# One recurrence step for four heads instead of two groups of two, 16-row products side by side, full value products first

## The chip, the cores and the metric

The kernel runs on one core of a Trainium2 chip. The metric is the device time of one execution in microseconds. Engines: PE (TensorE, the matrix products), PEld (its weight loads), DVE (VectorE), ACT (ScalarE), POOL (GpSimd) and SP (SyncE, which issues the loads of the weights).

## The reference: what is computed

A decoder trunk of two layers on 256 tokens plus 16 learned ones put ahead (272 in all), 1024 wide, float32. A layer is a half-step SwiGLU, a token-mixing part of two branches, and another half-step SwiGLU. The branches are latent attention with 8 heads and a gated linear recurrence (HGRN2) with 4 heads of 128 x 128. The change touches both branches, the second above all:

```python
def step(S, inp):
    qt, kt, vt, gt = inp
    b = jnp.cumsum(gt, axis=2)
    diff = b[:, :, :, None, :] - b[:, :, None, :, :]
    decay = jnp.exp(jnp.where(causal[:, :, None], diff, NEG_BIG))
    attn = jnp.einsum('bhtk,bhtsk,bhsk->bhts', qt, decay, kt) * scale
    o = jnp.einsum('bhts,bhsv->bhtv', attn, vt) + \
        jnp.einsum('bhtk,bhkv->bhtv', qt * jnp.exp(b) * scale, S)
    b_last = b[:, :, -1:, :]
    S = jnp.exp(b_last[:, :, 0, :])[..., None] * S + \
        jnp.einsum('bhsk,bhsv->bhkv', kt * jnp.exp(b_last - b), vt)
    return S, o
...
o = o * lax.rsqrt(jnp.mean(o * o, axis=-1, keepdims=True) + EPS) * norm_w.astype(f32)
gate = jax.nn.silu(g_in.astype(f32)).reshape(B, L, HG_HEADS, HG_VDIM)
return (o * gate).reshape(B, L, HG_WIDTH).astype(dt)
```

## The kernel before, in words

Activations lie feature-major: 128 features on the partitions, 272 tokens along them. In the last layer the 16 learned tokens are no longer needed as queries, and most work there runs on 256 columns.

Every weight is read from memory in float32 and split into an exact high and low part: ACT casts the high part (`wh`, L144), DVE subtracts (`wl`, L145). A wide product is three matrix products per contraction step (`mm3`, L163 to L165), so one output tile of 128 x 272 with 8 steps takes 24. The pieces of weights are prepared two ahead of their use. The other products, in the recurrence and in attention, are plain float32; in the trace one of them counts as two passes of PE.

PSUM has two rings of four tiles, `mm` (wide products) and `aux` (the rest). A tile is given out in the order in which the program asks, so a fifth request waits for the first one's readers.

`mix` (L399 on) is the token-mixing part. It is written as Python generators, dealt out by hand: each `yield` ends a step, and the loops at its end take a step of one, then of another. The recurrence inputs come first (`gq`, `gk`, `gf` for queries, keys and forget factors, two tiles each, one per group of two heads). Then:

- `halving(gr)`, one for each group `gr` of two heads, forms the decayed products by halving. For block sizes 1, 2, 4, 8, 16 `blocks` (products inside 32-token blocks, L714, and for the 16 learned tokens L718) and for 32 and 64 `halves` (L740) multiply keys and queries. Then DVE multiplies half of the queries and of the keys by the totals (L765, L767) before the next size. A last step forms the products between the two tiles of 128 tokens and with the 16 learned tokens (L778, L782). The results are gathered in `at`, `am` and `amm`. That is nine steps for each group.
- `outputs()` multiplies them with the values, head by head: a 16-row product into the 16 learned tokens (L798, not in the last layer), a 16-row product into the other 256 (L799), and two full-array products (L800, L801). Then it squares (L803), sums the squares over each head's features (L811), takes the square root on ACT and the reciprocal on DVE (L284, L285 of `rsqrt`), spreads the factors with one 32-row product for each head (L819), multiplies (L821) and splits (L168, L169).
- `attention()`, head by head, takes scores (L643), maximum, exponential (L648) and transposes (L661 to L663), the transposes of one head behind the scores of the next; at the end, two by two, the products with the values: one of full width (L684) and four that are 64 columns wide (L688), for each pair of heads.

The order around the change: while the four gate products run, one recurrence step follows each; so too for the four steps of `heads()` (attention's queries, keys and values); then `weave` goes round by round: a step of attention, a wide product, a step of the recurrence. The two groups take turns:

```python
rec = chain(alternate(halving(0), halving(1)), outputs())
for _ in tiles(4, cq, done_g):
    pump()
    next(rec)
...
for _ in weave("awr", a=attention(), r=rec, w=rest):
    pass
```

With 18 steps of halving and 5 of outputs, the recurrence takes 23 steps: 4, 4, and 15 rounds of the weave. Which instruction then stands where on an engine is set by a scheduler, which keeps roughly to the order of the program and lets others pass where its estimate says that one would wait.

Of the kernel before, what the change touches and what calls it, by code (L numbers as in the profile page):

```python
# [18 lines left out]
P = 128  # L19
# [3 lines left out]
NM = 16  # L23
# [29 lines left out]
def trunk(ctx: ExitStack, tc: tile.TileContext, a: dict):  # L53
# [28 lines left out]
    # a unit's pieces: (its number, contraction steps, columns)  # L82
# [67 lines left out]
    # the next piece, as a list over its contraction steps  # L150
# [33 lines left out]
    at = [T([P, 2, 3, P], F32, "at", 2) for _ in range(2)]  # L184
    for t in at:
        GP.memset(t, 0.0)
# [22 lines left out]
    # lower bounds of the forget gates, by a softmax over the layers  # L209
# [71 lines left out]
    # in steps, so that other work can stand between them  # L281
# [15 lines left out]
    # two or more output tiles; the last contraction step of all of them comes last  # L297
# [57 lines left out]
    # the last one, token-major, with the norm of the output  # L355
    def ffn_out(norm, c):
# [8 lines left out]
        for hf in range(2):  # L365
            pst = [PS(), PS()]
            for k0 in range(0, NF, 2):
                w = piece()
                for t in range(2):
# [6 lines left out]
                    for k in range(4 if k0 == 0 else 0):  # L376
                        E.matmul(pst[t][:, k * P:(k + 1) * P], h[4 * hf + k][:, slice(*TOK[1 + t])], ident,
                                 start=False, stop=False)
            for t in range(2):
                sq = T([P, 512], F32, "gq", 2)  # L380
                sq = S.activation(out=sq, in_=pst[t], func=AF.Square, accum_out=fm[:, hf, t:t + 1])
            for t in range(2):
                o = T([P, 512], F32, "gk" if hf else "gf", 2)
# [15 lines left out]
    def mix(l, norm, nxt):  # L399
# [12 lines left out]
        # rms_norm(r p) = p rsqrt(mean(p p) + EPS / (r r)), with 1 / (r r) from the outer norm  # L412
# [18 lines left out]
        # latent queries, latent keys and values (each with its norm), the shared rotary key  # L431
# [43 lines left out]
        def heads():  # L475
            kpe = st["kpe"]
            # queries
# [25 lines left out]
            # keys and values  # L503
# [40 lines left out]
        # recurrence inputs  # L544
# [9 lines left out]
        gq = [T([P, 2, L], F32, "gq", 2) for _ in range(2)]  # L554
        gk = [T([P, 2, L], F32, "gk", 2) for _ in range(2)]
# [59 lines left out]
        def attention():  # L615
# [66 lines left out]
            for pr in range(4):  # L682
# [10 lines left out]
                if pr % 2:  # L693
                    yield
# [297 lines left out]
```

## Time and profile before

| | |
|---|---|
| median of 3 runs | 1233.23 us (1232.86 to 1233.68) |
| span of the profiled execution | 1232.4 us |
| PE busy | 1216.2 us |
| DVE busy | 870.1 us |
| ACT busy | 643.7 us |
| instructions | 24345 |
| TensorE clock granted | 0.999 of full speed (2.4 GHz) |

The profiled execution's own time is its span, from its first instruction to its last, with a start and an end around it that the profile doesn't show; the median of the runs is 0.8 us above the span. In the timelines the start of an instruction is the safe number. The ends of PE's products are modelled and overlap, so what a product costs is read from its start to the next one's start.

### The profile page before, as it was taken

The page shows a single profiled execution, that of the slowest core. Times are in us where ns is not written, and L with a number is a line of the kernel's source. Part 1 is how long each engine was busy: PE and PEld are TensorE (multiplying, and loading weights), DVE is VectorE, ACT ScalarE, POOL GpSimd, SP SyncE. Part 2 cuts the span into 40 slices and gives each one's busy share as a digit, 9 for nine tenths or more (in the row PEclk, how much of TensorE's full clock was granted, in tenths as well). Part 3 has the DMA queues.
Part 4 walks back from the last instruction along what each step waited for, and adds up shares of the span by engine and source line. Part 5 has one row for each costly group of instructions (what it writes and reads, how often), then busy time and mean ns, then how long its engine had stood idle before and what let it go on. Part 6 is the DMA issues. An engine that isn't in the chain of part 4 may idle for free.

```text
span 1232.4 us, 24345 instructions
## 1 busy us (share of the span) xinstructions
PE 1216.2 (99%) x10210; PEld 1175.0 (95%) x10210; DVE 870.1 (71%) x1585; ACT 643.7 (52%) x1073; POOL 8.6 (1%) x28
## 2 busy tenths in 40 slices
PE   7999999999999999999999999999999999999997
PEld 6999999999988999999999999999998899999986
DVE  5877755787866877776558776558869586977743
ACT  5544444566774644444445444445776655545442
POOL 0000000000000000000000000000000000000000
PEclk9999999999999999999999999999999999999999
DMA  7645555545332545646555546555454345555651
GB/s 225 204 149 196 177 179 178 173 142 158 122 134 86 189 141 168 201 148 211 163 165 174 183 160 197 187 156 173 140 168 138 120 138 172 191 172 186 206 188 52
DMA packets 188781, 203.50 MB, mean 165 GB/s; under 512 B 3348, under 2 KB 176480, under 8 KB 188672
## 3 DMA queue, kind: packets, MB, share of 16 engines
q1 hardware_dynamic: 188272, 201.36, 50.4%
q8 instruction: 80, 1.31, 0.4%
q10 hardware_dynamic: 400, 0.60, 0.1%
q14 instruction: 29, 0.24, 0.1%
HBM read 200.89 MB, written 1.05 MB: 164 GB/s over the span
## 4 chain that ended last, share of the span: by engine, by line
PE 96%; ACT 2%; DVE 1%; DMA 1%; issue 0%; SPq 0%; POOLq 0%; POOL 0%
PE pmm L163 21%; PE pmm L164 21%; PE pmm L165 21%; PE paux L164 7%; PE paux L165 7%; PE paux L163 7%; PE pmm L373 2%; PE pmm L374 2%; PE pmm L375 2%; PE paux L643 1%; PE paux L714 1%; PE paux L688 1%; DMA raw<-x 1%; ACT wh L144 0%; ACT act L501 0%; PE paux L800 0%
## 5 line engine op out<-in xcount | busy, mean ns | idle before, releaser
L144 ACT CAST wh<-raw 128x1024 fp32r<-128x1024 f32 (+3 forms) x398 | 398.4, 1006 | 388.7 <-PE pmm L164 263.0
L145 DVE TENSOR_TENSOR wl<-raw,wh 128x1024 fp32r<-128x1024 f32 (+3 forms) x398 | 464.4, 1170 | 172.5 <-ACT wh L144 170.7
L163 PE MATMUL pmm<-x,wh 128*128 128x272 f32 (+1 forms) x1312 | 381.1, 291 | 0.7 <-ACT act L513 0.7
L165 PE MATMUL pmm<-x,wl 128*128 128x272 f32 (+1 forms) x1312 | 375.8, 287 | 0.0
L164 PE MATMUL pmm<-x,wh 128*128 128x272 f32 (+1 forms) x1312 | 375.6, 286 | 0.0
L163 PEld LDWEIGHTS pmm<-x,wh 128*128 128x128 f32 x1312 | 246.8, 188 | 3.0 <-ACT act L513 1.0
L164 PEld LDWEIGHTS pmm<-x,wh 128*128 128x128 f32 x1312 | 247.0, 188 | 0.9
L165 PEld LDWEIGHTS pmm<-x,wl 128*128 128x128 f32 x1312 | 246.4, 188 | 0.2
L163 PE MATMUL pmm<-act,wh 128*128 128x272 f32 (+1 forms) x836 | 239.8, 287 | 0.0
L164 PE MATMUL pmm<-act,wh 128*128 128x272 f32 (+1 forms) x836 | 239.1, 286 | 0.0
L165 PE MATMUL pmm<-act,wl 128*128 128x272 f32 (+1 forms) x836 | 238.9, 287 | 0.0
L163 PE MATMUL paux<-x,wh 128*128 128x272 f32 (+1 forms) x704 | 201.1, 286 | 0.0
L164 PE MATMUL paux<-x,wh 128*128 128x272 f32 (+1 forms) x704 | 201.1, 286 | 0.0
L165 PE MATMUL paux<-x,wl 128*128 128x272 f32 (+1 forms) x704 | 201.1, 286 | 0.0
L163 PEld LDWEIGHTS pmm<-act,wh 128*128 128x128 f32 x836 | 157.3, 188 | 1.0 <-issue 0.8
L164 PEld LDWEIGHTS pmm<-act,wh 128*128 128x128 f32 x836 | 157.5, 188 | 0.4 <-issue 0.4
L165 PEld LDWEIGHTS pmm<-act,wl 128*128 128x128 f32 x836 | 157.0, 188 | 0.5 <-issue 0.3
L163 PEld LDWEIGHTS paux<-x,wh 128*128 128x128 f32 x704 | 132.8, 189 | 0.0
L164 PEld LDWEIGHTS paux<-x,wh 128*128 128x128 f32 x704 | 132.6, 188 | 0.0
L165 PEld LDWEIGHTS paux<-x,wl 128*128 128x128 f32 x704 | 132.5, 188 | 0.0
L168 ACT CAST act<-tmp 128x272 fp32r<-128x272 f32 (+1 forms) x88 | 36.5, 415 | 124.4 <-DVE tmp L317 124.4
L313 DVE TENSOR_TENSOR tmp<-pmm,rstd 128x272 f32<-128x272 f32 (+1 forms) x88 | 38.3, 435 | 50.9 <-PE pmm L165 50.6
(239 smaller groups left out, 1058.9 us busy)
## 6 DMA issues: line engine op xcount, KB each, us to landing
raw<-ffn_w_gu SPq DMA_DIRECT2D x86, 1024.0 KB, 5.3
raw<-w_in SPq DMA_DIRECT2D x36, 1024.0 KB, 5.2
raw<-ffn_w_down SPq DMA_DIRECT2D x34, 1024.0 KB, 5.2
raw<-ffn_w_down SPq DMA_DIRECT2D x12, 768.0 KB, 4.9
raw<-w_out SPq DMA_DIRECT2D x8, 1024.0 KB, 5.4
raw<-w_proj_attn SPq DMA_DIRECT2D x4, 1024.0 KB, 5.0
raw<-w_proj_rec SPq DMA_DIRECT2D x4, 1024.0 KB, 5.0
raw<-ffn_w_gu SPq DMA_DIRECT2D x4, 512.0 KB, 9.0
```

What stands on the lines that cost most here:

```text
L144: S.copy(out=hw, in_=x)
L145: V.tensor_tensor(out=lw, in0=x, in1=hw.bitcast(F32), op=ALU.subtract)
L163: E.matmul(ps, wh, xh, start=start, stop=False)
L164: E.matmul(ps, wh, xl, start=False, stop=False)
L165: E.matmul(ps, wl, xh, start=False, stop=stop)
L168: S.copy(out=hi_tile[:, c], in_=src)
L313: V.tensor_tensor(out=gt[:, c], in0=pg[:, c], in1=r[:, c], op=ALU.mult)
L373: E.matmul(pst[t], ah[:, ts_], wh, start=k == 0, stop=False)
L374: E.matmul(pst[t], al[:, ts_], wh, start=False, stop=False)
L375: E.matmul(pst[t], ah[:, ts_], wl, start=False, stop=k == NF - 1)
L643: E.matmul(ps[:, 0:n], qs[hd][0:DQK, TOK[i + 1][0]:TOK[i + 1][1]], kT[hd][0:DQK, 0:n], start=True, stop=True)
L688: E.matmul(ps[j * 64:j * 64 + 64, 16 + i * P:L], vt[1 + i][:, hd * 64:hd * 64 + 64], pts[hd][:, i * 256:256 + i * P], start=False, stop=i ...
```

## The change

Four things are done. `halving` handles all four heads in one step: `gq`, `gk`, `gf`, `at` and the small tiles hold four heads, a visit to `blocks` or `halves` issues the products of four heads, and the instructions of DVE, ACT and POOL behind them are as many as for one group before, on tiles twice as large. The recurrence then has 14 steps in place of 23. `outputs` issues the 16-row products of all four heads first, into four tiles at once (two of `aux`, two of `mm`), and then the full-array ones head by head. In attention two full-width value products come first, and then the eight narrow ones. The last norm's scratch tiles are slices of one tile, since `gq`, `gk` and `gf` have another shape now; the comments are gone.

```diff
-    at = [T([P, 2, 3, P], F32, "at", 2) for _ in range(2)]
-    for t in at:
-        GP.memset(t, 0.0)
+    at = T([P, G, 3, P], F32, "at")
+    GP.memset(at, 0.0)
...
-        gq = [T([P, 2, L], F32, "gq", 2) for _ in range(2)]
-        gk = [T([P, 2, L], F32, "gk", 2) for _ in range(2)]
-        gf = [T([P, 2, L], F32, "gf", 2) for _ in range(2)]
+        gq, gk, gf = (T([P, G, L], F32, n) for n in ("gq", "gk", "gf"))
...
-            for pr in range(4):
-                ps = PS("aux")
-                E.matmul(ps[:, cq], vt[0][:, pr * P:(pr + 1) * P], pmt[:, cq], start=True, stop=False)
-                for i in range(2):
-                    for j in range(2):
...
+            for p2 in range(2):
+                prs = [(2 * p2 + i, PS("aux")) for i in range(2)]
+                for pr, ps in prs:
+                    E.matmul(ps[:, cq], vt[0][:, pr * P:(pr + 1) * P], pmt[:, cq], start=True, stop=False)
+                for pr, ps in prs:
+                    for i in range(2):
+                        for j in range(2):
...
                 ps = PS("aux")
-                pv = ps[:, 0:P].rearrange("p (j t c) -> p j t c", j=2, t=2)
-                for j in range(2):
+                pv = ps[:, 0:2 * P].rearrange("p (g t c) -> p g t c", g=G, t=2)
+                for g in range(G):
                     for ti in range(2):
                         for b in range(4):
                             bs = slice(TOK[2 - ti][0] + 32 * b, TOK[2 - ti][0] + 32 * b + 32)
-                            E.matmul(pv[32 * b:32 * b + 32, j, ti], k[:, j, bs], q[:, j, bs], start=True, stop=True)
+                            E.matmul(pv[32 * b:32 * b + 32, g, ti], k[:, g, bs], q[:, g, bs], start=True, stop=True)
...
                 V.tensor_tensor(out=qv[:, :, :, 1], in0=qv[:, :, :, 1],
-                                in1=first.unsqueeze(3).broadcast_to([P, 2, nq, b]), op=ALU.mult)
+                                in1=first.unsqueeze(3).broadcast_to([P, G, nq, b]), op=ALU.mult)
...
             og, sqs = [], []
+            pss = [PS(t) for t in ("aux", "aux", "mm", "mm")]
+
             for g in range(G):
-                gr, j = divmod(g, 2)
+                ms = slice(32 * g, 32 * g + NM)
+                if not last:
+                    E.matmul(pss[g][:, 0:NM], gv[0][ms], amm[ms], start=True, stop=True)
+                E.matmul(pss[g][:, NM:L], gv[0][ms], am[ms], start=True, stop=False)
+            for g in range(G):
                 gs = slice(g * P, (g + 1) * P)
-                ms = slice(32 * g, 32 * g + NM)
-                ps = PS("aux")
-                if not last:
-                    E.matmul(ps[:, 0:NM], gv[0][ms], amm[ms], start=True, stop=True)
-                E.matmul(ps[:, NM:L], gv[0][ms], am[ms], start=True, stop=False)
-                E.matmul(ps[:, NM:L], gv[1][:, gs], at[gr][:, j, 1:3], start=False, stop=False)
-                E.matmul(ps[:, 144:L], gv[2][:, gs], at[gr][:, j, 0], start=False, stop=True)
+                ps = pss[g]
+                E.matmul(ps[:, NM:L], gv[1][:, gs], at[:, g, 1:3], start=False, stop=False)
+                E.matmul(ps[:, 144:L], gv[2][:, gs], at[:, g, 0], start=False, stop=True)
...
-        rec = chain(alternate(halving(0), halving(1)), outputs())
+        rec = chain(halving(), outputs())
```

How it moves instructions, at two places (the lines are those of each kernel; the changed one's are a few lower). First, PE in the first layer, where the recurrence's outputs are formed; `gv` are the values, `at`, `am` and `amm` the decayed products. Before, for heads 0 and 1:

```order
L798 MATMUL paux_4712<-amm_2545,gv_427_2539 128x16
L799 MATMUL paux_4712<-am_2542,gv_427_2539 128x256
L800 MATMUL paux_4712<-at_69,gv_2540 128x256
L801 MATMUL paux_4712<-at_69,gv_2541 128x128
L798 MATMUL paux_4721<-amm_2545,gv_427_2539 128x16
L799 MATMUL paux_4721<-am_2542,gv_427_2539 128x256
L800 MATMUL paux_4721<-at_69,gv_2540 128x256
L801 MATMUL paux_4721<-at_69,gv_2541 128x128
```

Now, in the same step; the full-array products of heads 2 and 3 follow in the next one, behind a wide product:

```order
L793 MATMUL paux_4181<-amm_2539,gv_423_2534 128x16
L794 MATMUL paux_4181<-am_2537,gv_423_2534 128x256
L793 MATMUL paux_4182<-amm_2539,gv_423_2534 128x16
L794 MATMUL paux_4182<-am_2537,gv_423_2534 128x256
L793 MATMUL pmm_4183<-amm_2539,gv_423_2534 128x16
L794 MATMUL pmm_4183<-am_2537,gv_423_2534 128x256
L793 MATMUL pmm_4184<-amm_2539,gv_423_2534 128x16
L794 MATMUL pmm_4184<-am_2537,gv_423_2534 128x256
L798 MATMUL paux_4181<-at_69,gv_2535 128x256
L799 MATMUL paux_4181<-at_69,gv_2536 128x128
L798 MATMUL paux_4182<-at_69,gv_2535 128x256
L799 MATMUL paux_4182<-at_69,gv_2536 128x128
```

The 16-row products (before L798 and L799, now L793 and L794) of all four heads stand together ahead of the full-array ones, in four tiles, where they stood alternately with them.

Second, ACT in the first layer, where the root of the outputs' norm is taken (`rsqrt`, before L284, now L283). Before, in the stretch behind attention's last exponential (L860 is the sigmoid of the merge gates):

```order
L860 ACTIVATE act_4779<-act_4779 128x272
L803 ACTIVATE tmp_4786<-paux_4781 128x272
L803 ACTIVATE tmp_4795<-paux_4790 128x272
L284 ACT_TABLE_LOAD
L284 ACTIVATE tmp_4843<-tmp_4820 128x272
L144 CAST wh_4926<-raw_4924 128x1024
```

Now, between the exponentials (L645) of attention's heads 3 and 4; L662 copies transposes, L650 scales a head's second tile:

```order
L662 COPY ptt_4296<-paux_4292 128x384
L645 ACTIVATE pm_4274,sm_4038<-paux_4276,sm_4038 128x144
L645 ACTIVATE pm_4275,sm_4038<-paux_4284,sm_4038 128x272
L650 ACTIVATE pm_4275<-pm_4275,sm_4038 128x256
L144 CAST wh_4423<-raw_4362 128x1024
L283 ACT_TABLE_LOAD
L283 ACTIVATE tmp_4394<-tmp_4334 128x272
L645 ACT_TABLE_LOAD
L645 ACTIVATE pm_4337,sm_4038<-paux_4339,sm_4038 128x144
```

The root moved from behind attention into its middle, and a second table load follows it, back to the exponential.

## Rows read from the trace of the kernel before

**Rows 1.** The page, busy time by engine: us, share of the span, instructions.

```profile
PE 1216.2 (99%) x10210; PEld 1175.0 (95%) x10210; DVE 870.1 (71%) x1585; ACT 643.7 (52%) x1073; POOL 8.6 (1%) x28
```

**Rows 2.** The page, the chain that ended last, share by engine.

```profile
PE 96%; ACT 2%; DVE 1%; DMA 1%; issue 0%; SPq 0%; POOLq 0%; POOL 0%
```

**Rows 3.** Timeline of PE, layer 0, first visit to `blocks`: start, us, line, shape, count.

```profile
271.31 0.29 PE L165 MATMUL pmm<-x,wl 128*128 128x272 f32 x1
...
272.80 0.29 PE L165 MATMUL pmm<-x,wl 128*128 128x272 f32 x1
273.01 0.46 PE L714 MATMUL paux<-gq,gk 128*32 128x32 f32 x32
273.29 0.24 PE L718 MATMUL paux<-gq,gk 128*32 128x16 f32 x4
...
273.69 0.29 PE L164 MATMUL pmm<-x,wh 128*128 128x272 f32 x1
```

**Rows 4.** Timeline of PE, layer 0, output products of heads 0 and 1.

```profile
369.04 0.39 PE L801 MATMUL paux<-at,gv 128*128 128x128 f32 x2
369.35 0.39 PE L798 MATMUL paux<-amm,gv 16*128 16x16 f32 x2
369.60 0.67 PE L799 MATMUL paux<-am,gv 16*128 16x256 f32 x2
370.20 0.70 PE L800 MATMUL paux<-at,gv 128*128 128x256 f32 x2
370.74 0.38 PE L801 MATMUL paux<-at,gv 128*128 128x128 f32 x2
370.96 0.62 PE L684 MATMUL paux<-act,vt 128*128 128x272 f32 x2
```

**Rows 5.** Timeline of PE, layer 0, four 32-row products in four row groups.

```profile
389.28 0.74 PE L819 MATMUL paux<-act,cst 32*128 32x272 f32 x8
389.95 0.39 PE L164 MATMUL pmm<-act,wh 128*128 128x272 f32 x1
```

**Rows 6.** Timeline of PE, layer 0, value products of attention.

```profile
361.53 0.73 PE L684 MATMUL paux<-act,vt 128*128 128x272 f32 x2
362.19 0.87 PE L688 MATMUL paux<-ptt,vt 128*64 128x256 f32 x8
362.99 0.73 PE L684 MATMUL paux<-act,vt 128*128 128x272 f32 x2
```

**Rows 7.** Windows of 10 us, layer 0: PE, PEld, DVE, ACT, POOL busy (instructions), clock, DMA.

```profile
270.00:280.00 10.00, 10.00 (x144) 9.58 (x144) 7.47 (x17) 4.82 (x14) 0.00 (x0) 1.00 0.34 107
...
320.00:330.00 10.00, 10.00 (x136) 9.25 (x136) 9.81 (x34) 6.73 (x15) 0.34 (x2) 1.00 0.42 122
...
370.00:380.00 10.00, 10.00 (x64) 7.39 (x63) 3.67 (x7) 2.94 (x6) 0.00 (x0) 1.00 0.01 2
```

**Rows 8.** Groups of DVE by line: busy us, mean ns; idle before.

```profile
L285 DVE RECIPROCAL tmp<-tmp 128x272 f32<-128x272 f32 (+1 forms) x12 | 21.8, 1820 | 1.9 <-ACT tmp L284 1.8
...
L765 DVE TENSOR_TENSOR gq<-gq,tb 128x256 f32<-128x256 f32 (+1 forms) x24 | 10.2, 424 | 0.8 <-PE paux L740 0.7
...
L821 DVE SCALAR_TENSOR_TENSOR act<-paux,cols,act 128x272 f32<-128x272 f32 (+1 forms) x8 | 3.6, 486 | 0.8 <-PE paux L819 0.8
...
L746 DVE TENSOR_TENSOR gq<-gq,gf 128x544 f32<-128x544 f32 (+1 forms) x4 | 2.8, 698 | 0.0
```

**Rows 9.** Timeline of ACT, layer 0: the table load ahead of the square root.

```profile
380.88 1.28 ACT L284 ACT_TABLE_LOAD   x1
382.18 0.43 ACT L284 ACTIVATE tmp<-tmp 128x272 f32<-128x272 f32 x1
```

**Rows 10.** Waits of PE in the mixing stages: us in total, times, longest.

```profile
PE paux L662 <- ACT pm L653: 0.8, 1, 0.8
...
PE pmm L163 <- ACT act L513: 0.7, 1, 0.7
PE paux L643 <- ACT act L514: 0.7, 1, 0.7
```

More of the change, by code (lines that the diff above doesn't have):

```diff
@@ L378, in ffn_out @@
                                  start=False, stop=False)
+            sqs, os = (T([P, 2, 512], F32, n) for n in ("gq", "gk" if hf else "gf"))
             for t in range(2):
-                sq = T([P, 512], F32, "gq", 2)
-                sq = S.activation(out=sq, in_=pst[t], func=AF.Square, accum_out=fm[:, hf, t:t + 1])
+                sq = S.activation(out=sqs[:, t], in_=pst[t], func=AF.Square, accum_out=fm[:, hf, t:t + 1])
             for t in range(2):
-                o = T([P, 512], F32, "gk" if hf else "gf", 2)
+                o = os[:, t]
                 r = fm[:, 2, t:t + 1]
@@ L572, in done_q @@
             S.activation(out=s[:, cq], in_=z[:, cq], func=AF.Sigmoid)
-            V.scalar_tensor_tensor(out=gq[g // 2][:, g % 2, cq], in0=z[:, cq], scalar=P ** -0.5,
+            V.scalar_tensor_tensor(out=gq[:, g, cq], in0=z[:, cq], scalar=P ** -0.5,
                                    in1=s[:, cq], op0=ALU.mult, op1=ALU.mult)
@@ L739, in halves @@
                         for o in starts:
-                            E.matmul(pv[o:o + b, j, ti], k[:, j, t0 + o:t0 + o + b],
-                                     q[:, j, t0 + o + b:t0 + o + 2 * b], start=True, stop=True)
+                            E.matmul(pv[o:o + b, g, ti], k[:, g, t0 + o:t0 + o + b],
+                                     q[:, g, t0 + o + b:t0 + o + 2 * b], start=True, stop=True)
                 for o in starts:
@@ L771, in halving @@
                 yield
-            km = T([P, 2, 32], F32, "km", 2)
-            V.tensor_tensor(out=km, in0=k[:, :, 0:32], in1=tb[:, :, 0:1].broadcast_to([P, 2, 32]), op=ALU.mult)
+            km = T([P, G, 32], F32, "km", 1)
+            V.tensor_tensor(out=km, in0=k[:, :, 0:32], in1=tb[:, :, 0:1].broadcast_to([P, G, 32]), op=ALU.mult)
             ps = PS("aux")
             pmx = PS("aux")
-            for j in range(2):
-                E.matmul(ps[:, j * P:(j + 1) * P], k[:, j, 16:144], q[:, j, 144:272], start=True, stop=True)
+            for g in range(G):
+                E.matmul(ps[:, g * P:(g + 1) * P], k[:, g, 16:144], q[:, g, 144:272], start=True, stop=True)
             for i in range(2):
-                for j in range(2):
-                    o = 64 * gr + 32 * j
-                    E.matmul(pmx[o:o + 32, i * P:(i + 1) * P], km[:, j] if i else k[:, j, 0:32],
-                             q[:, j, 16 + i * P:144 + i * P], start=True, stop=True)
-            S.copy(out=A[:, :, 2, :], in_=ps[:, 0:256].rearrange("p (j c) -> p j c", j=2))
-            S.copy(out=am[hs], in_=pmx[hs, 0:256])
+                for g in range(G):
+                    E.matmul(pmx[32 * g:32 * g + 32, i * P:(i + 1) * P], km[:, g] if i else k[:, g, 0:32],
+                             q[:, g, 16 + i * P:144 + i * P], start=True, stop=True)
+            S.copy(out=A[:, :, 2, :], in_=ps.rearrange("p (g c) -> p g c", g=G))
+            S.copy(out=am, in_=pmx[:, 0:256])
             yield
```

48 lines of the change are left out of this document (23 added, 25 removed).

## The prediction

> **What bounds the kernel now.** Read the busy times first: PE is busy for 1216.2 of 1232.4 us [rows 1]; the other engines have room on the whole. The chain that ended last says the same, PE 96% [rows 2]. So a change pays only where PE issues for a shorter time, or waits less; an instruction saved on DVE or ACT pays nothing by itself. Then read PE's timeline in the two mixing stages (about 270 to 392 us and 880 to 1000 us), start to start, since the modelled ends overlap. Twelve wide products (three per contraction step, 272 columns) take 272.80 - 271.31 = 1.49 us, 0.124 each [rows 3]. What stands between them are small products, and there a start-to-start gap shows more than streaming: whenever PE goes from full-array products to ones on 32-column, 64-column or 16-row parts and back, it pays. Last read the load of DVE by stretch: 7.5 of 10 us while the gate products run, 9.8 in the rounds of attention, 3.7 where the recurrence's outputs stand now [rows 7]. PE waits little there: 0.7 twice for ACT's key copies, and 0.8 once for a transpose's input [rows 10].
>
> The profiled execution is the base of the sum: its span is 1232.4 us, and the median of the runs is 1233.23; I add 0.8 at the end.
>
> **Recurrence in one step for four heads.** The count of products is the same; the 18 visits per layer become 9. One visit now: from the last wide product before it (272.80) to the second behind it (273.69) 0.89 us, less two wide products, 0.64 [rows 3]. Of that, 32 passes take 0.28 (273.01 to 273.29) [rows 3]. A visit for four heads adds 32 passes and costs about 0.64 + 0.28 = 0.92 in place of 1.28. That is 0.36 per pair. In the last layer, which has no 16-column products, the visit is shorter, and for blocks of 32 and 64 tokens and the totals the added passes run on fewer columns at a time, so I take 0.29 per pair: 9 pairs x 2 layers x 0.29 = **5.2 us**. Bounds: 0, if the added passes cost a visit each time; 6.5, at 0.36 throughout.
>
> DVE has half as many instructions, but not half the time: 544 elements take 0.70 us, two instructions of 256 or 272 take 0.85 [rows 8]. The doubled steps now stand one behind the other in the four gate products and in the heads. There a step brings two multiplications and a masked copy, some 1.0 us more per round of 4 us; DVE is idle for 2.5 of 10 us [rows 7], 1.0 per round, so it just fits. I cost it at nothing; if the cover is gone, each of six rounds per layer lengthens by at most the 1.0. Pool's copies and the larger memset come long before they are needed.
>
> **16-row products side by side.** Now each head of the first layer has 0.25 (16 columns) + 0.60 (256 columns, with the way back to the full array) + 0.54 + 0.22, with 0.31 for the last where a 16-row product follows [rows 4]: 1.70, in the last layer without the first, 1.45. Four heads and two layers: 12.6 us. Afterwards four 16-row products stand in four row groups and four tiles. The nearest row is the spread of the head factors: four products of 32 rows and 272 columns take 0.67 together [rows 5], where one product of that width takes 0.47 on the full array (0.22 for 128 columns, scaled) [rows 4]. So they run together. I take 0.67, plus 0.25 once for the 16-column ones. The full products cost 0.22 per 128 columns, 0.66 per head, as no change of shape stands between them. With 0.1 for the one change into row groups: 3.7 and 3.4 us, 7.1 in all, **5.5 us** saved. Bounds: 1.3, if they run one by one; 6.0, if the 16-column ones cost nothing.
>
> **Full value products first.** 361.53 to 362.19 is 0.66 for one full product, of which 0.47 is streaming; the four half-width ones behind it take 0.80 [rows 6], of which about 0.63 is streaming. With two full ones and then eight half ones, one change each way goes, 0.19 + 0.17, at four places: **1.4 us**. Bounds 0 and 1.5.
>
> Together PE saves **12.1 us**.
>
> **What moves.** Before, recurrence steps reached into round 15 behind the start of attention, and the square root, the reciprocal and the norm products fell where DVE has 6 of 10 us free. Now the steps are 14, eight of them before attention starts, and the last five fall into rounds 2 to 6 of attention, DVE's full stretch. Out of these rounds go eight steps with two multiplications of 0.42 [rows 8]. In come per layer a reciprocal of 1.82, four products of 0.49, and 12 plain operations of 0.42 [rows 8], 8.9 us, lumped into two rounds. A round of PE is 24 wide products, 3.0, and one head's scores and transposes, some 1.05 by the columns; with the recurrence's visit, about 0.5 where the shape changes anyway, 4.6. DVE's own work in it is 4.6 x 0.98 [rows 7] less 1.3 of recurrence (two multiplications, a masked copy), 3.2. In the round of the norm products DVE gets 3.2 + 4 x 0.49 + 4 x 0.42 = 6.9 us against PE's 4.05 + 0.67: late by 2.2. In the round of the reciprocal ACT gets two table loads (to the square root and back to the exponential) of 1.28 [rows 9] and the root's 0.43 on top of some 3.1 [rows 7], 6.1 against PE's 5.2: late by 0.9. What is late next: the norm products take all four aux tiles, and the score products behind them on PE wait until DVE frees two; then maximum, exponential and transposes of that head. Part of this 3.1 us is covered, because a head's transposes are asked for a round later and wide products can stand between. I take two thirds, 2.1 per layer, less the old 0.8 which belonged to the same chain: **3.4 us** back. Bounds: 0 less 0.8, and 6.2. The two waits for key copies stay [rows 10].
>
> About the swap the Trainium skill, in "ScalarE: Activation LUTs", section "What ACT_TABLE_LOAD costs", says that each switch of sets costs a load of 1283 ns and a drain of about 1380 ns. The load agrees; the drain does not, as the root starts at 382.18, right where the load ends [rows 9]. By the page's price the two swaps per layer would take 2.76 us more on ACT, and the sum would rise by up to 5.5 us.
>
> The sum: 1232.4 - 12.1 + 3.4 = 1223.7, plus 0.8: **1224.5 us**.
>
> **The rivals.**
> - The waits don't come (wide products cover the lumps): 1232.4 - 12.1 - 0.8 + 0.8 = 1220.3. For it: PE's order puts wide products ahead of the late transposes. Against it: the aux tiles.
> - The 16-row products don't run side by side: 4.2 us less gain, 1228.7. For it: two of them stand on one row group, one behind the other. Against it: rows 5.
> - Doubled visits cost what two cost, so the first part doesn't do what it says: 5.2 less, 1229.7. Against it: 0.28 for 32 passes [rows 3].
> - The swap drains ACT, by a gap behind each load: 5.5 more, 1230.0. Rows 9 show no gap.
> - **Slower**: the norm work inside attention is paid in full. The place is the score products behind the norm products; the price 8.9 us of DVE per layer, 17.8, on 12.1 saved and 0.8 added: 1232.4 - 12.1 + 17.8 + 0.8 = 1238.9. It decides once the new waits pass 12.1 us, over 6 per layer. Against it: as much halving work leaves the same rounds.
>
> **How the numbers follow.** Forecast 0.55 (1221.5 to 1228), no waits 0.17, one by one 0.13, doubled visits 0.06, drain 0.03, slower 0.06. 0.2%, about what a measurement of this kernel can tell from no change, is 2.5 us: under 1230.8 counts as faster. The forecast and the first three rivals lie there but for their upper ends: faster 0.88, within 0.06, slower 0.06. The range, 1219 to 1230.5, takes in the cases on the side of a gain and leaves out the slower one and the upper ends.
>
> **What would show it.** Right: 9 recurrence visits per layer, of about 0.9 us; four 16-row products within about 1 us; two full value products in a row; PE's busy time near 1204; new waits of 2 us or so per layer behind the four norm products. Wrong: 16-row products 0.6 apart; PE waiting more than 6 us per layer for DVE's norm products or for ACT's table loads; or PE stalls among the gate products, where DVE would be the bound.

## The result, and the profile after

The changed kernel takes **1220.88 us** (1220.78 to 1221.88, four runs), the kernel before beside it 1233.3 us (1232.86 to 1233.68, four runs): 12.4 us less, a ratio of 0.9898 with an interval of 0.9886 to 0.9911. The profiled execution has a span of 1218.8 us and a time of 1220.78 us. The page of the kernel after, busy time and the chain by engine (to be read against [rows 1] and [rows 2]):

```profile
PE 1203.2 (99%) x10210; PEld 1170.0 (96%) x10210; DVE 866.9 (71%) x1522; ACT 645.5 (53%) x1067; POOL 8.7 (1%) x19
...
PE 96%; DVE 2%; ACT 1%; DMA 0%; issue 0%; SPq 0%; POOLq 0%; POOL 0%
```

PE still sets the time; it is busy for 13.0 us less with the same 10210 products. The chain has 2% of DVE now where it had 2% of ACT.

A second measure is used below, because medians of this size carry about a microsecond that has nothing to do with the change. The first 2082 products of PE are the same in every kernel here, and yet the first recurrence visit starts between 271.5 and 273.1 us in the kept traces: later where the wide products go over later from 0.23 us apart to 0.12 (15.0 to 18.5 us from the start), or where the first input is late. From the start of that visit to PE's last product the kernel before takes 952.4 us and the changed one 939.3, **13.1 us less**. This stretch is called the traced stretch; each run has one trace.

**The shapes.** PE's timeline in layer 0, kernel after: the first recurrence visit, the output products, one of the two value visits (start, us, line, tiles, shape, count):

```profile
272.42 0.29 PE L165 MATMUL pmm<-x,wl 128*128 128x272 f32 x1
272.63 0.73 PE L711 MATMUL paux<-gq,gk 128*32 128x32 f32 x62
...
273.38 0.39 PE L163 MATMUL pmm<-x,wh 128*128 128x272 f32 x1
273.61 0.29 PE L164 MATMUL pmm<-x,wh 128*128 128x272 f32 x1
...
327.02 0.29 PE L793 MATMUL paux<-amm,gv 16*128 16x16 f32 x2
...
327.26 0.47 PE L794 MATMUL paux<-am,gv 16*128 16x256 f32 x2
327.29 0.47 PE L794 MATMUL pmm<-am,gv 16*128 16x256 f32 x2
327.56 0.39 PE L794 MATMUL paux<-am,gv 16*128 16x256 f32 x2
327.59 0.39 PE L794 MATMUL pmm<-am,gv 16*128 16x256 f32 x2
327.90 0.70 PE L798 MATMUL paux<-at,gv 128*128 128x256 f32 x2
328.44 0.38 PE L799 MATMUL paux<-at,gv 128*128 128x128 f32 x2
...
338.80 0.67 PE L809 MATMUL paux<-tmp,ones 128*32 128x272 f32 x8
339.39 0.39 PE L640 MATMUL paux<-act,act 96*128 96x144 f32 x1
...
364.25 1.08 PE L682 MATMUL paux<-act,vt 128*128 128x272 f32 x4
365.26 1.52 PE L687 MATMUL paux<-ptt,vt 128*64 128x256 f32 x16
366.71 0.39 PE L163 MATMUL pmm<-x,wh 128*128 128x272 f32 x1
```

A four-head visit is 273.61 - 272.42 less two wide products, 0.94, where the pair of visits took 2 x 0.64 [rows 3]. Eight 16-row products take 327.90 - 327.02 = 0.88 for four heads, where one head's took 0.25 + 0.60 [rows 4]. Two full and eight half value products take 2.46 us (364.25 to 366.71) with one change each way, where 361.53 to 362.99 was half of that work in 1.46 [rows 6].

**The waits.** The waits of PE in the mixing stages, kernel after: us in total, times, longest.

```profile
PE paux L640 <- DVE act L819: 1.1, 2, 0.6
PE paux L737 <- DVE gk L764: 0.6, 2, 0.4
PE pmm L163 <- DVE act L605: 0.6, 2, 0.3
PE pmm L165 <- DVE wl L145: 0.4, 2, 0.2
```

None of the waits of [rows 10] is left, and four of another kind stand in their place, 2.7 us together, all for DVE. The first is the one behind the norm products; the other three belong to one step, the recurrence's 32-token step (`halves`, L737) in the round of the keys. PE's timeline there, kernel after, and below it DVE's and GpSimd's:

```profile
302.45 0.57 PE L737 MATMUL paux<-gq,gk 128*32 128x32 f32 x24 [0.22 <-DVE gk L764]
303.25 0.64 PE L165 MATMUL pmm<-act,wl 128*128 128x272 f32 x3 [0.23 <-DVE wl L145]
303.82 0.32 PE L737 MATMUL paux<-gq,gk 128*32 128x32 f32 x8
304.41 0.39 PE L163 MATMUL pmm<-act,wh 128*128 128x272 f32 x1 [0.27 <-DVE act L605]
```

```profile
300.71 0.89 DVE L762 TENSOR_TENSOR gq<-gq,tb 128x512 f32<-128x512 f32 x1
301.52 0.88 DVE L764 TENSOR_TENSOR gk<-gk,tb 128x512 f32<-128x512 f32 x1
302.32 1.68 DVE L145 TENSOR_TENSOR wl<-raw,wh 128x512 fp32r<-128x512 f32 x2
...
306.54 0.68 DVE L762 TENSOR_TENSOR gq<-gq,tb 128x512 f32<-128x512 f32 x1
...
300.62 2.85 POOL L753 COPY at<-cb 32x256 f32<-32x256 f32 x4 [297.85 <-DVE cb L723]
```

Three wide products stand in the middle of the visit, so it pays its changes of shape twice. The windows of the kernel after, in layer 0, for this round and for the round of the norm products (PE, PEld, DVE, ACT, POOL busy, clock, DMA) show DVE full in both.

```profile
296.00:306.00 10.00, 9.28 (x153) 8.46 (x152) 10.00 (x21) 9.12 (x19) 2.67 (x4) 1.00 0.44 117
340.00:350.00 10.00, 10.00 (x80) 9.67 (x82) 10.00 (x28) 8.27 (x17) 0.00 (x0) 1.00 0.32 106
```

Part of that load is GpSimd's doing. Beside its copies (300.62) four DVE instructions on 128 x 512 elements in a row, the two multiplications and two subtractions, take 0.88 to 0.89 us each, where the same sizes take 0.68 to 0.69 without them: 0.8 us per layer, at the very place where PE waits 0.7 us in layer 0 and 0.9 in the last. No run takes the copies away, so it is not shown whether PE would wait without them.

### The profile page after: what moved, and what is told of

Read it like the earlier page. It is cut to its first block, busy times and chain, and to the rows that moved or that the text cites. A ratio compares the mean times of both kernels' runs of the same rounds, so it can differ in the third digit from the quotient of the medians.

```text
span 1218.8 us, 24265 instructions
## 1 busy us (share of the span) xinstructions
PE 1203.2 (99%) x10210; PEld 1170.0 (96%) x10210; DVE 866.9 (71%) x1522; ACT 645.5 (53%) x1067; POOL 8.7 (1%) x19
## 3 DMA queue, kind: packets, MB, share of 16 engines
q8 instruction: 80, 1.31, 0.5%
## 4 chain that ended last, share of the span: by engine, by line
PE 96%; DVE 2%; ACT 1%; DMA 0%; issue 0%; SPq 0%; POOLq 0%; POOL 0%
PE pmm L163 22%; PE pmm L164 21%; PE pmm L165 21%; PE paux L164 7%; PE paux L165 7%; PE paux L163 7%; PE pmm L372 2%; PE pmm L373 2%; PE pmm L374 2%; PE paux L640 1%; DVE wl L145 1%; PE paux L711 1%; DMA raw<-x 0%; PE paux L687 0%; PE pmm L376 0%; PE paux L682 0%
## 5 line engine op out<-in xcount | busy, mean ns | idle before, releaser
L164 PE MATMUL pmm<-x,wh 128*128 128x272 f32 (+1 forms) x1312 | 376.0, 287 | 0.0
L164 PEld LDWEIGHTS pmm<-x,wh 128*128 128x128 f32 x1312 | 247.1, 188 | 1.0
L164 PE MATMUL pmm<-act,wh 128*128 128x272 f32 (+1 forms) x836 | 238.8, 286 | 0.0
L164 PE MATMUL paux<-x,wh 128*128 128x272 f32 (+1 forms) x704 | 201.1, 286 | 0.0
L164 PEld LDWEIGHTS pmm<-act,wh 128*128 128x128 f32 x836 | 157.4, 188 | 0.0
L164 PEld LDWEIGHTS paux<-x,wh 128*128 128x128 f32 x704 | 132.6, 188 | 0.0
```

The lines of the kernel that those rows point to most:

```text
L164: E.matmul(ps, wh, xl, start=False, stop=False)
```

## The experiments

Each group of runs was timed against the kernel before on its own chip (1233.0 to 1233.4 us). Differences between two runs of this list are differences of medians, without an interval of their own; the traced stretch stands beside them where the two disagree.

**The three parts alone.** First the value products only: of the diff above, on the kernel before, the loop in `attention` and nothing else.

> The kernel before with the third part of the change alone: two full-width value products first, then the eight narrow ones. Shape theory (PE's gain comes from fewer changes between full-array and narrow products): each of the four places takes 2.5 to 2.6 us in place of 2.9, so the time falls by about 1.5 us and PE's busy time with it. Rival, waits theory (the gain of the whole change comes from moving the recurrence off attention's rounds, so that PE waits less): no change, within 0.3 us.

1232.04 us, ratio 0.999 (0.9981 to 0.9999): 1.0 us less, with up to 2.3 in the interval; in the traced stretch 1.2. Each of the four places shrinks by 0.34 to 0.36 us, from 6.32 to 5.96 at one of them. Shape, as expected.

Second the output products only, on the kernel before:

```diff
+            pss = [PS(t) for t in ("aux", "aux", "mm", "mm")]
+            for g in range(G):
...
+                E.matmul(pss[g][:, NM:L], gv[0][ms], am[ms], start=True, stop=False)
             for g in range(G):
...
-                E.matmul(ps[:, NM:L], gv[0][ms], am[ms], start=True, stop=False)
+                ps = pss[g]
```

> The kernel before with the second part alone: the 16-row products of all four heads first, into two aux and two mm tiles; the halving stays in two groups. Shape theory: the 16-row products stand within about 0.9 us in the first layer and 0.65 in the last, in place of 3.4 and 2.4, and the time falls by about 5.7 us. Waits theory: less than 1 us. A third outcome, that two of the four mm tiles held over a wide product make PE wait for a tile: the fall is smaller by as much as the waits that then show ahead of wide products.

1229.83 us, ratio 0.9972 (0.9961 to 0.9983): 3.2 us less, in the traced stretch 3.6. The 16-row products stand side by side as in the changed kernel, 0.89 for the eight of layer 0. Part of that gain is lost again behind attention, at two places. The product for the sum of squares comes right behind the last square there, is split in two by a wide product, and pays two changes of shape: 0.8 us per layer. And behind the norm products PE waits for DVE's splits (L164 <- DVE act L169, 0.6 us in two waits), which it reaches earlier now.

Third the recurrence for four heads only: the changed kernel with the old loops in `attention` and `outputs`.

> The changed kernel with the outputs head by head and the value products pair by pair as before, so the four-head halving and its earlier steps alone. Shape theory: a fall of 3.6 us from the visits, 1.1 from the sum of squares which no longer waits for ACT's last square, and 0.8 of new waits, in all about 4 us below the kernel before. Waits theory: this part carries most of the whole change, a fall of 8 us or more.

1227.81 us, ratio 0.9953 (0.994 to 0.9967): 5.2 us less, in the traced stretch 5.9; the waits of [rows 10] are gone, and the four waits of the changed kernel are there. So this part alone exchanges the waits. The three parts give 1.0 + 3.2 + 5.2 = 9.4 us alone and 12.4 together; each interval reaches 1.1 to 1.7 us to either side, so the times don't settle the difference. The traced stretches do say that there is one, 10.8 against 13.1: alone, the output products lose what the paragraph above tells, and in the changed kernel the sum of squares is in one piece and no wait for L169 is left.

**The sum of squares.** In the kernel before, its product L811 takes 1.14 us, start to start; in the changed kernel L809 takes 0.59. PE's timeline in the kernel before, and the wait that its weight loads (PEld) have there:

```profile
380.36 1.20 PE L811 MATMUL paux<-tmp,ones 128*32 128x272 f32 x8
381.50 0.40 PE L163 MATMUL pmm<-act,wh 128*128 128x272 f32 x1
...
PEld paux L811 <- ACT tmp L803: 0.8, 2, 0.4
```

One more `yield` ahead of it, in the kernel before:

```diff
+            yield
             ss = PS("aux")
```

> The kernel before with one more step between the output products and the product that sums their squares, nothing else. If the 1.14 us of that product was mostly a wait for ACT's last square, it takes about 0.6 now and the time falls by about 1 us. If it is what four products in column groups take, it stays at 1.1 and the time stays within 0.3 us.

PE's timeline of this run:

```profile
380.67 0.67 PE L812 MATMUL paux<-tmp,ones 128*32 128x272 f32 x8
381.27 0.39 PE L163 MATMUL pmm<-act,wh 128*128 128x272 f32 x1
```

The product takes 0.60: half of the 1.14 was a wait for ACT's last square, as the first of the two outcomes had it. But the time does not fall: 1232.93 us, ratio 0.9998 (0.9989 to 1.0006), and the traced stretch is 952.4 us in both. PE gains 0.5 us per layer at this place and loses it some 14 us later, where the first products behind the norm products wait for DVE's splits (L164 <- DVE act L169, 0.2 us at 394.78). So behind attention PE can't use the gain: what comes later there is the chain of root, reciprocal, norm products and splits.

**The tiles of the norm products.** The changed kernel with

```diff
-            pss = [PS("aux") for _ in range(G)]
+            pss = [PS(t) for t in ("mm", "mm", "aux", "aux")]
```

> The changed kernel, with one edit: the four products that spread the head factors (L817) take two tiles of mm and two of aux, where they took four of aux. In the changed kernel the score products behind them (L640) wait for DVE's L819, 1.1 us of PE's idle time at two places, and 2.0 us of the weight loads'. Theory A, the prediction's: the wait is for the ring of aux tiles; then it goes, and the time falls by 1.1 to 2.0 us, to about 1219.4 (ratio to the changed kernel 0.9987, to the kernel before 0.989), and no row L640 <- DVE act L819 is left. Theory B: DVE is late with everything in this round, so the wait only moves, to the next tile of mm or to the transposes L658: within 0.5 us of 1220.9, and a new row of 0.5 us or more appears.

1224.66 us (1223.59 to 1225.43), ratio 0.9931 (0.9918 to 0.9945): **3.8 us slower** than the changed kernel, in the traced stretch 4.1, so neither theory holds. The waits of PE, its timeline in the last layer, and the windows:

```profile
PE pmm L817 <- DVE act L288: 2.9, 2, 1.6
PE paux L658 <- DVE act L819: 1.3, 2, 0.8
```

```profile
952.07 0.48 PE L817 MATMUL pmm<-act,cst 32*128 32x256 f32 x2 [1.62 <-DVE act L288]
...
955.51 0.41 PE L163 MATMUL pmm<-x,wh 128*128 128x256 f32 x1
955.73 0.41 PE L164 MATMUL pmm<-x,wh 128*128 128x256 f32 x1
```

```profile
952.00:954.50 2.50, 1.90 (x14) 1.16 (x15) 2.50 (x6) 0.80 (x2) 0.00 (x0) 0.82 0.05 20
954.50:957.00 2.50, 2.50 (x12) 2.50 (x13) 2.15 (x8) 1.27 (x4) 0.00 (x0) 0.50 0.88 326
```

The wait behind the norm products went from L640 to L658, as theory B had it. The larger one is new: with tiles of mm the norm products stand right behind the score round, and PE waits for the root's result (L288). In the changed kernel, 16 wide products more stand ahead of L817; only the tiles were edited, so it is the aux ring, which the prediction counted as the price, that put this cover in front of the norm products. Without the cover the two waits are 4.2 us. Behind them, in the last layer, the granted clock falls to 0.50, 1.2 GHz, with wide products 0.21 apart, and a part of the 3.8 us is that: the next run, with the same waits at the same place, keeps the clock. The profiled execution is the fastest of the five, at a mean granted clock of 0.998; the other four have 0.996.

**The place of the outputs.** The changed kernel with the outputs held until attention has its four results:

```diff
+        def hold():
+            while len(oa) < 4:
+                yield
...
-        rec = chain(halving(), outputs())
+        rec = chain(halving(), hold(), outputs())
```

> The changed kernel, with one edit: the steps from the recurrence's outputs on are held until attention's last value products are issued, as they stood before, so that no square root, table load or norm product falls into attention's rounds. Theory A, from the trace: the early place costs almost nothing (waits of 1.1 us for L640) and gives back as much, since the product of the squares' sum (0.59 us early, 1.14 before) and the key-copy waits (1.4) were paid at the late place: the time is 1220.9 to 1223, none or up to 2 us slower than the changed kernel. Theory B, the prediction's term: the early place costs 2.1 us per layer less the old 0.8, 3.4 in all; then the late place is faster by about that, near 1217.5.

**1219.26 us** (1219.17 to 1219.42), ratio 0.9886 (0.9872 to 0.9899): 1.6 us less than the changed kernel, between the two theories. The intervals of the two ratios overlap, the runs don't. But of the 1.5 us between the two profiled executions (1220.78 and 1219.27) 1.0 lies ahead of the first recurrence visit (272.63 us against 271.64), where the two kernels are the same; the traced stretch is 938.8 us against 939.3, 0.5 less. The wait for L819 is gone, no wait of [rows 10] is back, and all 16 output products of a layer stand in one visit. So the early place costs 0.5 us by the traces and 1.6 at most by the medians, well under the prediction's 3.4, and the old waits did not depend on it.

**Four full value products first**, on the run with the norm tiles: one step for all four pairs.

```diff
-            for p2 in range(2):
-                prs = [(2 * p2 + i, PS("aux")) for i in range(2)]
+            for p2 in range(1):
+                prs = [(i, PS("aux")) for i in range(4)]
```

> The kernel of the run with the norm tiles in mm and aux, with one more edit: all four full value products of a layer stand first, then the sixteen half-width ones, in one step, where they stood two by two. One change of shape each way goes per layer: by the prediction's price of 0.36 us for the pair of changes, 0.7 us over two layers. Theory A: shape changes are priced as in the prediction, 0.3 to 0.9 us faster than that run, about 1218.8. Theory B: all four pairs' splits come later and the projection behind them waits for DVE: 0.5 to 3 us slower than that run, with a wait of the first products of the projection for L689 to L692's splits.

1223.19 us (1222.91 to 1224.08), ratio 0.9919 (0.9905 to 0.9932): 1.5 us less than the run it stands on, in the traced stretch 1.8. Start to start, less two wide products, the visits shrink from 2 x 2.57 to 4.78 us in layer 0 and from 2 x 2.50 to 4.67 in the last, 0.7 us together, the price of theory A, and there is no wait for the splits. The rest is the clock. PE's waits in the last layer are those of the run with the norm tiles, 1.62 and 0.58 us, and here the clock stays up behind them (the window that was at 0.50 there):

```profile
955.50:958.00 2.50, 2.50 (x22) 2.50 (x23) 2.50 (x9) 1.56 (x5) 0.00 (x0) 1.00 0.84 316
```

From the first norm product to the next score products it is 5.4 us here and 6.6 there: the low clock cost 1.2. So the norm tiles alone cost about 3.0 us, the traced stretch of this run plus the 0.7 that the value products save, against the changed kernel's.

**The 32-token step.** The changed kernel with the heads' other products first:

```diff
         for _ in heads():
-            next(rec)
             next(rest)
+            next(rec)
```

> The changed kernel, with one edit: in the four rounds of the heads, the round's other wide products are put ahead of the recurrence's step instead of behind it. In the changed kernel the 32-token step (L737) falls at 302.45 us and 906.95 us right behind DVE's two multiplications of 0.89 and 0.88 us; PE waits 0.2 and 0.4 us for gk, 0.2 twice for wl, 0.3 twice for the factor product L605, 1.6 us in all, and three wide products stand in the middle of the visit, which pays a second change of shape, about 1.0 us per layer. Theory A: the doubled multiplications of this one round ran out of cover, and the place is at fault; then the waits and the second visit go, 1.6 + 2.0 = 3.6 us, to about 1217.3 us (at least 2 us faster than 1220.9), and the visit is one of about 1.1 us. Theory B: DVE is full in this stretch whatever stands on PE; then the time stays within 1 us of 1220.9 and PE waits as long for wl or for the factors' products elsewhere between 290 and 320 us.

1222.58 us (1221.55 to 1224.05), ratio 0.991 (0.9895 to 0.9925): not faster, so theory A fails; 1.7 us slower by the medians, but the intervals and the runs overlap. The three waits for DVE are gone and the visit is whole, as theory A had it. In their place (waits of PE; its windows in this round):

```profile
PE pmm L163 <- ACT act L512: 2.4, 2, 1.3
...
PE pmm L530 <- ACT act L512: 1.0, 2, 0.5
```

```profile
304.00:306.60 2.60, 1.52 (x36) 1.22 (x37) 2.60 (x4) 2.51 (x7) 2.60 (x1) 1.00 0.94 324
306.60:310.20 3.60, 3.60 (x18) 3.56 (x17) 0.60 (x1) 3.46 (x10) 2.04 (x4) 0.54 0.87 278
```

PE waits 3.4 us in the two layers together for ACT's key copies, where the kernel before waited 1.4 [rows 10]. Behind the waits of layer 0 the clock falls, to 0.54; behind those of the last layer it does not. Two of the four runs have a mean granted clock of 0.999, both at 1221.55 us, and two 0.997, 1223.62 (the profiled one) and 1224.05. So this round is short of both engines: the four-head step only stood in front of ACT's wait.

**Two versions with that order.** Outputs held, four full value products first, and the other products first in the heads:

> A version meant to beat both: the changed kernel with the outputs held until attention's value products are issued (1219.3 us by itself), all four full value products first (0.7 us by the trace of the run with the norm tiles), and the other wide products ahead of the recurrence's step in the heads. Theory A of the run beside it: 1219.3 - 0.7 - 3.6 = 1215.0 us. Theory B: 1219.3 - 0.7 = 1218.6. If the parts share a cover (the splits of all four value pairs late, the squares behind them), more than 1219.

1224.25 us (1223.01 to 1226.76), ratio 0.9931 (0.9918 to 0.9943): 5.0 us slower than with the outputs held alone; of the outcomes expected only the last, more than 1219 us, fits. The same waits for L512, 3.4 us, are there, and in the profiled execution, the slowest of the five, the clock falls behind them in both layers; PE also waits 0.7 us for the splits (L169). The three edits do not add up, and what each loses beside the others was not taken apart. The second relieves ACT, by

```diff
-                    S.copy(out=kT[2 * pr + j][pe], in_=kpe[0:32])
+                    GP.tensor_copy(out=kT[2 * pr + j][pe], in_=kpe[0:32])
```

on the run with the other products first:

> The run with the other wide products first in the heads (1222.6 us), with one more edit: the eight copies of the rotary key (L513, 0.42 us each, 3.4 us of ACT per layer) go to GpSimd. In that run ACT is busy without a gap from 299.9 to past 309 us, PE waits 1.3 and 0.5 us for its copies L512, in both layers, and right behind the second wait twelve or more wide products stand 0.23 us apart in place of 0.124, at a granted clock of 0.54. Theory A: the key round is bound by ACT; 3.4 us less on ACT take both waits away, and with them the stretch of low clock: 3.4 us of waits and about 1.3 us of clock, to 1218 us or less, below the changed kernel's 1220.9. Theory B: the copies on GpSimd take 0.7 to 1.5 us each and come late, or DVE slows beside them; then PE waits for DVE's wl or factor products, or the score products for the keys: 1221 us or more.

1221.71 us (1220.61 to 1222.06), ratio 0.9904 (0.9887 to 0.992): 0.9 us less than without by the medians, not clear of noise. Waits of PE, and the second of the same windows:

```profile
PE pmm L163 <- ACT act L512: 1.6, 2, 0.9
...
PE pmm L530 <- ACT act L512: 0.6, 2, 0.3
```

```profile
306.60:310.20 3.60, 3.60 (x54) 3.47 (x55) 2.03 (x3) 1.71 (x5) 3.37 (x6) 1.00 0.76 230
```

The number is theory B's, but not its mechanism: the waits for ACT shrink from 3.4 to 2.2 us and the clock holds. They don't go: on ACT eight copies of the queries (L500, 3.41 us from 301.03) stand ahead of the key copies, which start at 304.45.

**GpSimd's copies with the outputs held**, with the other products first and without:

> The same two edits (other wide products first in the heads, rotary key copies on GpSimd) on the run with the outputs held behind attention (1219.3 us), value products two by two as in the changed kernel: a version meant to beat both. Theory A: the waits of the 32-token step (1.6 us) and its second visit (2.0) go and no wait for key copies comes in their place: 1215.7 us. Theory B: 1219 us or more, with new waits of PE as in the run beside it.

> The run with the outputs held behind attention (1219.3 us), with the rotary key copies on GpSimd alone, the recurrence's step ahead of the other wide products as in the changed kernel. PE's waits in this round are for DVE (gk L764, wl L145, factor products L605: 1.6 us, and the second visit, 2.0), not for ACT. Theory A: DVE is the bound there; with ACT relieved nothing changes, 1218.8 to 1219.6 us, and these waits stay. Theory B: DVE's lateness comes from ACT, whose casts (L144) feed DVE's L145; then the waits shrink and the time falls by 1 to 3 us.

1221.0 us (1220.51 to 1221.31), ratio 0.9901 (0.9886 to 0.9915), with the waits of the run before it, 2.2 us; theory A missed. And 1219.7 us (1219.29 to 1220.14), ratio 0.989 (0.9876 to 0.9905), with the three waits for DVE unchanged (0.6, 0.6, 0.4): there theory A holds but for 0.1 us: ACT's relief is worth nothing, and PE waits for DVE in this step (or for GpSimd's copies through DVE, which this run keeps). The lowest time of the study is that with only the outputs held, 1219.26 us; this one, 0.4 above it, has a traced stretch 0.1 us shorter, so the two can't be told apart.

All runs, us:

| run | median | traced stretch |
|---|---|---|
| kernel before | 1233.0 to 1233.4 | 952.4 |
| changed kernel | 1220.88 | 939.3 |
| value products only | 1232.04 | 951.1 |
| output products only | 1229.83 | 948.8 |
| recurrence only | 1227.81 | 946.4 |
| sum of squares later, kernel before | 1232.93 | 952.4 |
| norm tiles | 1224.66 | 943.4, low clock in one layer |
| outputs held | 1219.26 | 938.8 |
| norm tiles, four full value products first | 1223.19 | 941.7 |
| other products first | 1222.58 | 942.7, low clock in one layer |
| outputs held, four full first, other products first | 1224.25 | 945.8, low clock in both layers |
| other products first, GpSimd's copies | 1221.71 | 940.2 |
| the same, outputs held | 1221.0 | 940.1 |
| outputs held, GpSimd's copies | 1219.7 | 938.7 |

## Why the prediction was right, and where it was not

The forecast was 1224.5 us, the result 1220.9: a gain as forecast, inside the range, but the number is that of the first rival, that no waits come (1220.3). That is luck on the rival's side: new waits did come, 3.2 us of them, and nearly as much of the old ones went. Net of the old, the prediction put the waits at +3.4 us; the traces have +0.3.

To add up the two traces, the second wide product behind a visit less the one ahead of it, less two wide products, for all visits of both mixing stages; from the second norm product (L415, now L414) to the last steps of `mix` they shrink by 6.6 and 6.5 us, 13.0 together.

| | forecast | by the traces |
|---|---|---|
| recurrence visits, without waits | -5.2 | -5.1 |
| output products | -5.5 | -5.5 |
| value products | -1.4 | -1.4 |
| new waits, norm products and 32-token step | +4.2 | +3.2 |
| old waits gone | -0.8 | -2.9 |
| sum of squares | 0 | -1.1 |
| meta-token score products (L619), in one piece | 0 | -0.3 |
| sum | -8.7 | -13.1 |

The sum is firm; the split is less so, because many visits hold products of several kinds. If each product is charged with its own gap to the next one, the recurrence's come to -3.7 and the score products beside them to -1.8, together much the same.

- **The shapes were right.** The three terms hold to 0.1 us in this split; the value products alone, where nothing else moved, shrank by 1.4. The visit costs 0.94 where 0.92 was taken, and the nearest row for the four 16-row products, the head factors [rows 5], was the right one: 0.64 for four of 256 columns, from 327.26 to 327.90.
- **The step that failed** is "The two waits for key copies stay", and with it "less the old 0.8". All old waits went, with the changes of shape around them 2.9 us. The run with the recurrence alone has none of them either, so that part did it. The two for key copies were in the keys' round, short of ACT [rows 10]; now PE is held up there first, by DVE, and ACT is done when PE comes. The run with the other products first shows the wait underneath. The third, for the transposes (0.8), is in an attention round of the last layer, and the prediction had it go.
- **The new waits had nearly the forecast size, and half of it another place.** That 3.2 is near 4.2 is luck. Of the 6.2 us gross behind the norm products and the table loads, 1.6 came (1.1 of waiting, the rest around it). The lump on DVE is real: 4.2 us of waits when the cover is taken away, in the run with the norm tiles. But the wide products in front hid most of it; "I take two thirds" should have been about a quarter. (Of the terms behind it, PE's 5.2 us in the round of the reciprocal has no working, beside 4.6 for a round.) The other 1.6 is the 32-token step. There the prediction said of the doubled steps "I cost it at nothing", with a bound of 1.0 per round, and DVE's idle time was read at 270 to 280 us [rows 7], where it still fits, not in the keys' round, where DVE in layer 0 was busy for 9.9 of 10 us already. The window of the kernel before:

```profile
296.00:306.00 10.00, 9.23 (x135) 8.39 (x135) 9.88 (x27) 9.03 (x20) 0.00 (x0) 1.00 0.64 200
```

  It also put Pool's copies at nothing, since they come early enough; it left out that DVE runs slower beside them.
- **Not in the sum:** the sum of squares. Its 1.14 us in the kernel before held a wait for ACT's squares. PE's own list of waits names none there; the weight loads' list does (0.8 us in two waits), and so does the start-to-start gap. The prediction read neither at this place. In the kernel before its removal alone gave nothing, as the run above shows; in the changed kernel the gain stays.
- **The rival of the drain** falls: two table loads stand in one round of attention, each starts where ACT's work before it ends, and the work goes on where each ends. ACT's timeline of the kernel after:

```profile
339.84 1.28 ACT L283 ACT_TABLE_LOAD   x1
341.14 0.43 ACT L283 ACTIVATE tmp<-tmp 128x272 f32<-128x272 f32 x1
341.59 1.28 ACT L645 ACT_TABLE_LOAD   x1
342.88 0.38 ACT L645 ACTIVATE pm<-paux,sm 128x144 f32<-128x144 f32 x1
```

  The Trainium skill, in "ScalarE: Activation LUTs", section "What ACT_TABLE_LOAD costs", adds a drain of about 1380 ns to each switch; no such gap is here.
- **The base.** The 0.8 us between span and time joins two executions: in every run whose span and time are both on record they are 1.7 to 2.2 us apart. The profiled execution of the kernel before was one of its slower ones (span 1232.4; the others have 1230.4 to 1232.4), and its first input came late (PE waited 0.9 us for it, 0.3 in the changed kernel's). The sum does not suffer, as 1232.4 + 0.8 is the median; but spans differ by 13.6 us where medians differ by 12.4.

## What to carry to other kernels

Price a change of PE's order by start-to-start gaps of the nearest shapes; that held within a few tenths of a microsecond. Price its waits round by round: take DVE's and ACT's idle time from the very round in which the doubled or moved steps will stand, and ask of every old wait whether PE will still be early there. Look at every engine that works there, also at one that is nearly idle over the whole kernel, as GpSimd is. Before a ring of tiles is blamed for a wait, see what the wait lets pass in front: here its removal cost 3.8 us, some 3.0 without the fall of the clock. And before a difference of a microsecond between medians is given a cause, compare the traces from the first place where the kernels differ.

## What the runs showed of the hardware

- A wait of PE can cost more than itself. After gaps of 1.31 and 0.51 us (in the run with the other products first), or 1.62 and 0.53 (norm tiles), wide products ran 0.23 and 0.21 us apart in place of 0.12 for some 2 to 3.5 us, at a granted clock of 0.54 and 0.50, the lower of the two levels. But the gaps alone do not decide it: after 1.62 and 0.58 at the same place, in the run with four full value products first, the clock stayed at 1.00; after 1.12 and 0.52 in the last layer it fell in the run with three edits (1.12, 0.53) and held in that with the other products first. After 0.9 and 0.3 us it held. What else it takes is open.
- Products in different row groups interleave: each fp32 product runs in two passes, and the first passes of all four heads start before the second ones (327.26, 327.29, then 327.56, 327.59).
- DVE and GpSimd slow each other, and the one that started first came off better. The copies by GpSimd in the changed kernel and in the run with the other products first (shortest, median, longest, ns):

```profile
L753 POOL COPY at<-cb x8: 427/746/749, 300.6 to 907.2; 32x256 f32<-32x256 f32 x8
...
L753 POOL COPY at<-cb x8: 394/400/4772, 302.7 to 915.1; 32x256 f32<-32x256 f32 x8
```

  In the changed kernel the first copy starts at 300.62, just ahead of DVE's multiplication, and both take turns: 0.89 and 0.88 us for DVE (300.71, 301.52) in place of 0.68 (306.54), 0.75 for a copy in place of 0.40. In the other run DVE's L762 starts at 302.43 and the first copy at 302.69: DVE keeps its 0.69, the copy takes 4.76 us, until six DVE instructions in a row are through, and the three copies behind it take 0.39 to 0.40 each. The Trainium skill, in "GPSIMD Engine Reference", section "1. Specifications", names DVE instructions with two SBUF inputs among those that contend; these are such, and the trace agrees.
